# A two-layer float32 hybrid decoder: the indexer's queries and keys turned by VectorE and DRAM instead of TensorE, and four waits moved

## The chip, the cores and the metric

The kernel runs on one core of a Trainium2 chip. The metric is the device time of one execution in microseconds (us). Three runs of the kernel before gave 906.01, 906.24 and 907.55 us, a median of 906.24. The profile is of a further execution.

## The reference, cut to what matters

Two layers with an RMSNorm, one wide input projection, two kinds of attention heads, a gate and an output projection each. The sequence has 256 positions and the model 2048 columns. In layer 0 a small indexer with 16 heads of 64 columns (`iq`, `ik`) scores the keys of every query; the best 64 keys are what the heads of mixer A may attend to.

```python
def dsa_attention(q, k, v, iq, ik, iw):              # mixer A, layer 0
    dots = einsum('bqhd,bsd->bqhs', iqb, ikf) * IDX_DIM ** -0.5
    score = einsum('bqh,bqhs->bqs', iwb * IDX_HEADS ** -0.5, relu(dots))
    score = where(causal, score, -inf)
    _, sel = top_k(score, 64)
    ...                                              # softmax attention over the selected keys

def stick_breaking_attention(q, k, v):               # mixer C, layer 1
    z = einsum('bqhd,bshd->bhqs', qb, k) * HEAD_DIM ** -0.5
    log_1m = where(before, log_sigmoid(-z), 0.0)
    tail = cumsum(log_1m, axis=3, reverse=True) - log_1m
    w = where(before, exp(log_sigmoid(z) + tail), 0.0)
    return einsum('bhqs,bshd->bqhd', w, v)

def forgetting_attention(q, k, v, log_f):            # mixer D, layer 1
    c = cumsum(log_f, axis=1)
    logits = einsum(q, k) * HEAD_DIM ** -0.5 + (c[t] - c[s])
    return softmax(causal(logits)) @ v

def layer_even(x, norm_g, w_in, w_out):              # layer_odd likewise with C, D and log_f
    h = rmsnorm(x, norm_g)
    qa, ka, va, iq, ik, iw, qb, kb, vb, gate = split_cols(h @ w_in)
    qa, ka, iq, ik, qb, kb = rope of each            # halves turned against each other
    y = concat(dsa_attention(...), dilated_attention(...))
    return x + (y * silu(gate)) @ w_out
```

## The kernel before, in words

The program is a row of 39 jobs, each a projection of 256 tokens by up to 512 columns: B0, K, I0, I1, B1 to B3, A0 to A8, B4, B5 (layer 0's input), P0 to P3 (its output), C0, F1, G1, C2 to C7, D0 to D7, and Q0 to Q3. I0 and I1 are the indexer's queries, eight heads each; K holds the shared key and value of mixer A and the indexer's key. F1 and G1 together are head C1 and the forget gates.

A weight in float32 is split in two by ScalarE (`whi`, line 283) and VectorE (`wlo`, line 284), 128 x 1024 elements (a "half", two of the 16 blocks of 128 model columns) at a time, three halves ahead of TensorE, in four buffers each. TensorE then makes six 128 x 512 matmuls for each of the 16 blocks (lines 324, 325, 327): high by high, high by low, low by high, for both halves of the tokens. One such block is a **tick** of the program's clock (`tick`, `advance`).

All else is written as Python generators that say `yield n`: go on n ticks later. `start` sets one off when the projection it needs is done. So the order of the instructions of every engine is fixed when the program is built, and a step that is reached before its input is there makes its engine wait, with everything behind it.

Data is turned (tokens in partitions to tokens in columns) in two ways. `turn` (line 385) lets TensorE do it: a transpose of 128 x 128 each, into a PSUM tile `tp`, out of which ScalarE and VectorE copy. `far` (lines 410 to 432) goes another way: VectorE turns the 32 x 32 blocks of a tile (line 416), a DMA stores that to DRAM (line 424), and a second DMA loads it with the blocks in their places (line 426); its three numbers are the ticks before each of the three steps. The queues for these DMAs and for the weights (`raw`) are SyncE's.

The generators that matter here:

- `keys_a` (line 621) begins 4 ticks after K's projection. It rotates both keys; the indexer's key is copied to have it twice side by side (line 629), and `turn` is used on it (line 633). The key of mixer A goes through `far`, two blocks wide.
- `index` (line 648) rotates the queries of eight heads with `rotate`, and uses `turn` four transposes at a time for each half of the tokens (line 657): 8 transposes in I0 and 8 in I1. Then, one tick apart, 8 groups of products `s` (lines 442 to 444, 679, 680) of 3 or 4 matmuls, each followed by ScalarE's Relu (`rl`) and VectorE's sums (`score`).
- `best` (line 691) follows I1's `index`: 16 steps, 2 ticks apart, each taking the 8 largest scores and striking them out; then the mask `nbA` for mixer A's heads.
- `stick_head` (line 882), heads C0 to C7: products of q and k, four functions on ScalarE and VectorE, products with the triangle `tris`, then `z` (line 903), its exponential (904), the split `ph`, `pl` (lines 455, 456), and 4 ticks after the triangle's products `weigh_out` (line 486): products `o` of the weights with the values (442 to 444, 491).
- `forget` (line 845): log of the forget gates, and 13 ticks later its sums over positions (lines 859, 860), in the same single PSUM tile `s` that the heads use.
- `softmax_head` (line 528), heads B and D. The last of each kind (B5 and D7) have their inputs turned by TensorE.

Of the kernel before, what the change touches and what calls it, by code (L numbers as in the profile page):

```python
# [59 lines left out]
def _cols0(n):  # L60
    qa, ka, va, iq, ik, iw, qb, kb, vb, g = O0
    h = int(n[1:] or 0)
    if n == "K":
        p = [_inter(ka, HD), _run_of(va, 0), _inter(ik, DI), np.arange(iw, iw + NI)]
    elif n[0] == "I":
        p = [_inter(iq + (8 * h + i) * DI, DI) for i in range(8)]
    elif n[0] == "B":
        p = [_inter(qb + h * HD, HD), _inter(kb + h * HD, HD), _run_of(vb, h),
             (_run_of if h == HB - 1 else _gate_of)(g, HA + h)]
    else:  # L70
        p = [_inter(qa + h * HD, HD), _inter(qa + (h + 1) * HD, HD), _gate_of(g, h), _gate_of(g, h + 1)]
    return np.concatenate(p)
# [53 lines left out]

CW = 1792
RW = 1280


def _consts():
    q = np.arange(P)[:, None]
    k = np.arange(P)[None, :]
    f = np.float32
    tri = (q <= k).astype(f)
    one = np.ones((P, P), f)
    ntri = -(q >= k).astype(f)
    caus = np.where(k <= q, 0.0, BIG).astype(f)
    nmask = np.concatenate([caus, np.zeros((P, P), f), caus], 1)

    def dil(d):
        c = (d >= 0) & (d <= 128)
        c = c.astype(np.int64) + ((d >= 0) & (d % 4 == 0)) + ((d >= 0) & (d % 16 == 0))
        return np.where(c > 0, -np.log(np.maximum(c, 1).astype(np.float64)), BIG).astype(f)

    bmask = np.concatenate([dil(q - k), dil(q + P - np.arange(SEQ)[None, :])], 1)
    sm = np.where(q < k, 0.0, -BIG).astype(f)
    smask = np.concatenate([sm, np.zeros((P, P), f), sm], 1)
    return np.ascontiguousarray(np.concatenate([np.eye(P, dtype=f), tri, one, ntri, -one, nmask, bmask, smask], 1))


def _rope():
    f = np.float32
    pos = np.arange(SEQ).astype(f)

    def tab(dim):
        half = dim // 2
        inv = (f(10000.0) ** (-np.arange(half, dtype=f) / f(half))).astype(f)
        ang = pos[:, None] * inv[None, :]
        c, s = np.cos(ang).astype(f), np.sin(ang).astype(f)  # L160
        return np.repeat(c, 2, 1), np.stack([-s, s], -1).reshape(SEQ, dim)

    c, s = tab(HD)
    sc = f(-(HD ** -0.5))
    t = np.concatenate([c * sc, c, s * sc, s], 1).astype(f)
    ci, si = tab(DI)
    t = np.concatenate([t, ci, si], 1)
    return np.ascontiguousarray(t.reshape(NT, P, -1).transpose(1, 0, 2).reshape(P, -1))
# [5 lines left out]
def trunk(ctx, tc, x, xT, g1, w0, wo0, w1, wo1, bf, gf, consts, rope, out):  # L174
# [22 lines left out]
    ones = cons[:, 256:384]  # L197
    ntri = cons[:, 384:512]
    nones = cons[:, 512:640]
    nmask = cons[:, 640:1024]  # L200
    bmask = cons[:, 1024:1408]
    smask = cons[:, 1408:1792]
    ss = cp.tile([P, 3, NT, 5], F32, name="ss")
# [162 lines left out]
    def rotate(dst, src, cos, sin, r, m, swap=False):  # L366
# [15 lines left out]
        else:  # L382
            nc.gpsimd.tensor_tensor(dst, t1[:, 0:n], t2[:, 0:n], op=OP.add)  # L383

    def turn(srcs):
        pt = pa.tile([P, 512], F32, name="tp", tag="tp", bufs=2)
        for i, s in enumerate(srcs):
            nc.tensor.transpose(pt[:, i * P:(i + 1) * P], s, ident)  # L388
        return pt
# [14 lines left out]
    def arrived(t, n):  # L404

        return t.rearrange("p (i b c) -> p b i c", i=4, b=n)
# [121 lines left out]
    def softmax_head(qk, ticks, nb, v, u, rs, kt, last):  # L528
        uT = None if last else gate_turned(u)
        qk = yield from qk_turned(qk, ticks, last)  # L530
        pr, l = soft(qk, nb() if callable(nb) else nb)
        yield 2
        share(pr, factor(l, rs))
        yield 2 if last else 4
        pt = turn([pr[:, 0:P], pr[:, P:SEQ], pr[:, SEQ:384]])
# [87 lines left out]
    def keys_a(ps):  # L623
        kr = hp.tile([P, 512], F32, name="kr", tag="qk")
        for th in range(NT):
            rotate(kr[:, th * P:(th + 1) * P], ps[th][:, 0:P], rt[:, th, P:2 * P], rt[:, th, 3 * P:4 * P], 1, P)
            o = 256 + th * P
            rotate(kr[:, o:o + DI], ps[th][:, 256:320], rt[:, th, 512:576], rt[:, th, 576:640], 1, DI)
            nc.gpsimd.tensor_copy(kr[:, o + DI:o + P], kr[:, o:o + DI])
            nc.scalar.activation(vA[:, 1 - th, :], ps[1 - th][:, P:2 * P], AF.Copy, scale=r0[:, 1 - th:2 - th])  # L630
            nc.vector.tensor_scalar(iw[:, th, :], ps[th][:, 320:336], r0[:, th:th + 1], None, op0=OP.mult)
        yield 5
        pt = turn([kr[:, i * P:(i + 1) * P] for i in (2, 3)])
        nc.scalar.activation(ikh[:, 0:SEQ], pt[:, 0:256], AF.Copy)
        nc.vector.tensor_tensor(ikl[:, 0:SEQ], pt[:, 0:256], ikh[:, 0:SEQ].bitcast(F32), op=OP.subtract)
        for j in range(2):
            d = slice(j * DI, (j + 1) * DI)
            c = slice(SEQ + j * P, SEQ + (j + 1) * P)
            for t in (ikh, ikl):
                nc.gpsimd.tensor_copy(t[d, c], t[d, 0:P].bitcast(F32))  # L640
        yield from far([kr[:, 0:256]], kr[:, 0:256], 1, 2, 4)
        yield 5
        k = arrived(kr[:, 0:256], 2)
        nc.scalar.activation(quarters(kA), k[:, 0:1], AF.Copy)
        nc.scalar.activation(quarters(kAh), k, AF.Copy)
        nc.vector.tensor_tensor(quarters(kAl), k, quarters(kAh).bitcast(F32), op=OP.subtract)

    def index(ps, c):
# [4 lines left out]
        for th in range(NT):  # L653
            rotate(qr[th], ps[th], rt[:, th, 512:576], rt[:, th, 576:640], 8, DI)
        yield 3
        for th in range(NT):
            pt = turn([qr[th][:, i * P:(i + 1) * P] for i in range(4)])
            if th == 0:
                nc.scalar.activation(ih[:, 0], pt, AF.Copy)
                nc.vector.tensor_tensor(ih[:, 1], pt, ih[:, 0].bitcast(F32), op=OP.subtract)  # L660
            else:
                pq = pt.rearrange("p (a b) -> p a b", a=4)
                d = [slice(0, DI), slice(DI, P)]
                for j in range(2):
                    nc.scalar.activation(il[d[j], :, j], pq[d[j]], AF.Copy)
                for j in range(2):
                    nc.vector.tensor_tensor(il[d[1 - j], :, j], pq[d[j]], il[d[j], :, j].bitcast(F32), op=OP.subtract)
            yield 2
        for h2 in range(4):
# [174 lines left out]
    def forget(ps):  # L844
# [11 lines left out]
        nc.vector.scalar_tensor_tensor(flat(logf), flat(z), 0.0, flat(e), op0=OP.min, op1=OP.subtract)  # L856
        yield 13
        pc = pa.tile([P, 512], F32, name="s", tag="s", bufs=1)
# [23 lines left out]
    def stick_head(qk, v, uT, kt):  # L882
# [24 lines left out]
        cut((ph, pl), z[:, P:384])  # L907
        yield 4
        weigh_out(ph, pl, z[:, 0:P], v, uT, kt, True)
# [75 lines left out]
    for ji, (_, _, name, _) in enumerate(jobs):  # L985
# [8 lines left out]
        if name == "P0":  # L994
# [6 lines left out]
            tris = [tt[:, 0], tt[:, 1]]  # L1001
            nc.scalar.activation(tris[0], ntri, AF.Copy)
            nc.scalar.activation(tris[1], nones, AF.Copy)
        if name in ("D2", "D4"):
# [5 lines left out]
        elif k == "K":  # L1010
            start(delay(keys_a(ps), 4))
        elif k == "I":
# [53 lines left out]
```

## Time and profile before

| | |
|---|---|
| three runs | 906.01, 906.24, 907.55 us |
| the profiled execution, device time | 905.67 us |
| its span in the profile | 903.9 us |
| mean granted clock of TensorE, of full speed | 0.998 |
| TensorE matmul busy | 892.9 us, 99% |
| TensorE weight load busy (beside the matmuls) | 747.0 us, 83% |
| VectorE busy | 646.8 us, 72% |
| ScalarE busy | 475.0 us, 53% |
| GpSimd busy | 50.5 us, 6% |
| DMA | 194.2 MB, mean 215 GB/s |

How to read it: a matmul's own duration is its time from first to last element through the engine, and the next one starts before it ends. So what a matmul costs the stream is the distance from its start to the start of the next one, not its duration. In the timeline of an engine each row gives the start, the duration, the engine, the line, the instruction and, in brackets, how long the engine stood idle before it and for what. Rows of the same kind that follow each other are merged (x2, x3).

### The profile page before, as it was taken

How to read it: one execution, taken by the hardware profiler on the slowest of the kernel's cores; microseconds unless marked ns; L12 is line 12 of the kernel's file. 1: busy time of each engine (PE TensorE's matmuls, PEld its weight loads, DVE VectorE, ACT ScalarE, POOL GpSimd, SP SyncE). 2: the span in 40 equal slices, each digit the busy share in tenths (PEclk: the TensorE clock that was granted, in tenths of full speed). 3: DMA queues.
4: the chain of work that ended last, by engine and by line, in shares of the span. 5: the costliest groups of instructions: out<-in, count | busy, mean ns of one | idle time of the engine just before them, and what ended most of it. 6: DMA issues, size and time to landing. Idle time of an engine off the chain costs nothing.

```text
span 903.9 us, 11930 instructions
## 1 busy us (share of the span) xinstructions
PE 892.9 (99%) x4295; PEld 747.0 (83%) x4295; DVE 646.8 (72%) x1136; ACT 475.0 (53%) x834; POOL 50.5 (6%) x71
## 2 busy tenths in 40 slices
PE   9999999999999999999999999999999999999996
PEld 6988888888888888888897888888888888887886
DVE  7667888866777776666666777777787777776563
ACT  7645554554555455555455555555555555555440
POOL 0031100000000000000000000000000000001110
PEclk9999999999999999999999999999999999999999
DMA  9884455665555665666576655555676766664542
GB/s 358 333 292 145 182 210 184 227 228 203 201 206 202 215 222 186 233 233 233 165 273 240 208 202 193 206 211 195 211 254 222 238 218 216 205 199 180 188 185 93
DMA packets 67355, 194.20 MB, mean 215 GB/s; under 512 B 15952, under 2 KB 38624, under 8 KB 49376
## 3 DMA queue, kind: packets, MB, share of 16 engines
q1 hardware_dynamic: 65856, 190.14, 59.4%
q0 software_dynamic: 864, 2.12, 1.0%
q10 hardware_dynamic: 576, 1.19, 0.4%
q8 instruction: 33, 0.54, 0.2%
q14 instruction: 26, 0.21, 0.1%
HBM read 178.61 MB, written 14.82 MB: 214 GB/s over the span
## 4 chain that ended last, share of the span: by engine, by line
PE 82%; DVE 10%; ACT 4%; issue 3%; DMA 1%; POOL 0%; SPq 0%; POOLq 0%; DVEq 0%; ACTq 0%
PE pj L324 26%; PE pj L325 25%; PE pj L327 25%; DVE wlo L284 3%; DVE e L834 2%; ACT whi L283 1%; PE tp L388 1%; PE o L443 1%; PE s L504 1%; DVE far L416 1%; DMA w0yh<-in_w_in_dram 1%; PE o L491 1%; PE s L444 1%; PE s L443 1%; PE s L442 1%
## 5 line engine op out<-in xcount | busy, mean ns | idle before, releaser
L284 DVE TENSOR_TENSOR wlo<-raw,whi 128x1024 fp32r<-128x1024 f32 (+3 forms) x300 | 355.1, 1201 | 144.5 <-ACT whi L283 143.7
L324 PE MATMUL pj<-whi,xh 128*128 128x512 f32 (+3 forms) x992 | 381.0, 386 | 0.4 <-ACT whi L283 0.4
L325 PE MATMUL pj<-whi,xl 128*128 128x512 f32 (+3 forms) x992 | 376.5, 381 | 0.0
L283 ACT ACTIVATE whi<-raw 128x1024 fp32r<-128x1024 f32 (+3 forms) x300 | 299.6, 1024 | 85.3 <-PE pj L325 69.6
L327 PE MATMUL pj<-wlo,xh 128*128 128x512 f32 (+3 forms) x992 | 296.9, 381 | 0.1
L324 PEld LDWEIGHTS pj<-whi,xh 128*128 128x128 f32 x992 | 186.7, 188 | 33.3 <-ACT whi L283 1.4
L327 PEld LDWEIGHTS pj<-wlo,xh 128*128 128x128 f32 x992 | 183.4, 188 | 36.6 <-DVE wlo L284 0.8
L325 PEld LDWEIGHTS pj<-whi,xl 128*128 128x128 f32 x992 | 186.7, 188 | 32.0
L324 PE MATMUL pj<-whi,yh 128*128 128x512 f32 (+1 forms) x248 | 95.7, 386 | 0.0
L325 PE MATMUL pj<-whi,yl 128*128 128x512 f32 (+1 forms) x248 | 94.9, 383 | 0.0
L327 PE MATMUL pj<-wlo,yh 128*128 128x512 f32 (+1 forms) x248 | 76.6, 382 | 0.0
L512 ACT ACTIVATE sn<-sn,nm 128x128 f32<-128x128 f32 (+1 forms) x48 | 21.5, 449 | 62.6 <-DVE nm L510 62.6
L327 PEld LDWEIGHTS pj<-wlo,yh 128*128 128x128 f32 x248 | 46.6, 188 | 9.2
L324 PEld LDWEIGHTS pj<-whi,yh 128*128 128x128 f32 x248 | 46.7, 188 | 8.7
L325 PEld LDWEIGHTS pj<-whi,yl 128*128 128x128 f32 x248 | 46.6, 188 | 8.7
L455 ACT ACTIVATE yh<-uT 128x256 fp32r<-128x256 f32 (+1 forms) x27 | 12.4, 458 | 54.8 <-DVE uT L497 28.0
L548 ACT ACTIVATE sq<-xs 128x512 f32<-128x512 f32 x23 | 14.3, 623 | 28.9 <-DVE xs L773 26.9
L834 DVE RECIPROCAL e<-e 128x256 f32<-128x256 f32 x16 | 28.1, 1753 | 0.5
L383 POOL TENSOR_TENSOR qk<-rot,rot 128x256 f32<-128x256 f32 x16 | 11.9, 741 | 227.6 <-DVE rot L378 116.9
L456 DVE TENSOR_TENSOR yl<-uT,yh 128x256 fp32r<-128x256 f32 (+1 forms) x27 | 12.8, 475 | 14.3 <-ACT yh L455 14.3
L871 POOL DMA_DIRECT2D cb<-cTd x8 | 5.8, 722 | 252.2 <-DVE nb L876 223.7
L904 ACT ACTIVATE z<-z 128x384 f32<-128x384 f32 x8 | 4.2, 525 | 29.1 <-DVE z L903 29.1
(229 smaller groups left out, 739.6 us busy)
## 6 DMA issues: line engine op xcount, KB each, us to landing
raw<-in_w_in_dram SPq DMA_DIRECT2D x108, 1024.0 KB, 5.2
raw<-in_w_out_dram SPq DMA_DIRECT2D x32, 1024.0 KB, 4.9
fard<-far SPq DMA_DIRECT2D x38, 256.0 KB, 2.1
qk<-fard SPq DMA_DIRECT2D x25, 256.0 KB, 5.1
raw<-in_w_in_dram SPq DMA_DIRECT2D x4, 672.0 KB, 8.8
fard<-far SPq DMA_DIRECT2D x21, 128.0 KB, 3.7
uT<-fard SPq DMA_DIRECT2D x20, 128.0 KB, 5.0
raw<-in_w_in_dram SPq DMA_DIRECT2D x4, 528.0 KB, 3.8
```

Of the source, the lines that this page charges most:

```text
L283: nc.scalar.activation(hi, rw, AF.Copy)
L284: nc.vector.tensor_tensor(lo, rw, hi.bitcast(F32), op=OP.subtract)
L324: nc.tensor.matmul(o, a, wh, start=(kt == 0), stop=False)
L325: nc.tensor.matmul(o, b, wh, start=False, stop=False)
L327: nc.tensor.matmul(o, a, wl, start=False, stop=(kt == KT - 1))
L383: nc.gpsimd.tensor_tensor(dst, t1[:, 0:n], t2[:, 0:n], op=OP.add)
L443: nc.tensor.matmul(o, ah, bl, start=False, stop=False)
L455: nc.scalar.activation(dst[0], src, AF.Copy)
L456: nc.vector.tensor_tensor(dst[1], src, dst[0].bitcast(F32), op=OP.subtract)
L512: nc.scalar.activation(sn[:, s], sn[:, s], AF.Exp, scale=-1.0, bias=nm[:, th:th + 1], accum_out=l[:, th:th + 1])
L548: nc.scalar.activation(j, xs[:, th, c * 512:(c + 1) * 512], AF.Square, accum_out=ss[:, i, th, c:c + 1])
L834: nc.vector.reciprocal(e, e)
```

## The change

The indexer no longer uses `turn`. Its queries and its key take the way of `far`. For that, the columns of two heads (64 each) are interleaved by 16 in the weights, so that a tile of 128 columns holds a pair and the blocks come out in their places; the tables of the rotation are laid out likewise (128 columns in place of 64: the table `rt` grows by 128 KB, and the constants shrink by as much, two matrices fewer). The key, which has to stand in both halves of the pair, is rotated twice at once by a new function `rotate_twice`. The key of mixer A and that of the indexer go through one `far` of four blocks.

```diff
@@ _cols0
     elif n[0] == "I":
-        p = [_inter(iq + (8 * h + i) * DI, DI) for i in range(8)]
+        p = [_inter(iq + (8 * h + i) * DI, DI).reshape(4, 16) for i in range(8)]
+        p = [np.stack(p[i:i + 2], 1).reshape(-1) for i in range(0, 8, 2)]
...
-CW = 1792
-RW = 1280
+CW = 1536
+RW = 1536
...
+    def rotate_twice(dst, src, cos, sin):
+        t1 = hp.tile([P, 512], F32, name="rot1", tag="rt1")
+        t2 = hp.tile([P, 512], F32, name="rot2", tag="rt2")
+        wide = lambda a: a.rearrange("p (j a m) -> p j a m", j=4, a=2)
+        pair = lambda a: a.rearrange("p (j a m two) -> p j a m two", j=4, a=2, two=2)
+        sb = src.rearrange("p (j m) -> p j m", j=4).unsqueeze(2).to_broadcast([P, 4, 2, 16])
+        nc.vector.tensor_tensor(wide(t1[:, 0:P]), sb, wide(cos), op=OP.mult)
+        sw = src.rearrange("p (j m two) -> p j m two", j=4, two=2)[:, :, :, ::-1]
+        for a in range(2):
+            nc.vector.tensor_tensor(pair(t2[:, 0:P])[:, :, a], sw, pair(sin)[:, :, a], op=OP.mult)
+        nc.gpsimd.tensor_tensor(dst, t1[:, 0:P], t2[:, 0:P], op=OP.add)
@@ softmax_head
         pr, l = soft(qk, nb() if callable(nb) else nb)
-        yield 2
+        if not last:
+            yield 2
         share(pr, factor(l, rs))
-        yield 2 if last else 4
+        yield 4
@@ keys_a
-            rotate(kr[:, o:o + DI], ps[th][:, 256:320], rt[:, th, 512:576], rt[:, th, 576:640], 1, DI)
-            nc.gpsimd.tensor_copy(kr[:, o + DI:o + P], kr[:, o:o + DI])
+            rotate_twice(kr[:, o:o + P], ps[th][:, 256:320], rt[:, th, 512:640], rt[:, th, 640:768])
...
-        yield 5
-        pt = turn([kr[:, i * P:(i + 1) * P] for i in (2, 3)])
-        nc.scalar.activation(ikh[:, 0:SEQ], pt[:, 0:256], AF.Copy)
...
+        yield from far([kr], kr, 2, 2, 4)
+        yield 4
+        k = arrived(kr, 4)
+        nc.scalar.activation(quarters(ikh[:, 0:SEQ]), k[:, 2:4], AF.Copy)
...
-        yield from far([kr[:, 0:256]], kr[:, 0:256], 1, 2, 4)
-        yield 5
...
@@ index
         for th in range(NT):
-            rotate(qr[th], ps[th], rt[:, th, 512:576], rt[:, th, 576:640], 8, DI)
-        yield 3
+            rotate(qr[th], ps[th], rt[:, th, 512:640], rt[:, th, 640:768], 4, P)
         for th in range(NT):
-            pt = turn([qr[th][:, i * P:(i + 1) * P] for i in range(4)])
...
-            yield 2
+            start(far([qr[th]], qr[th], 2, 2, 4))
+        yield 12
+        hi, lo = (quarters(ih[:, j]) for j in range(2))
+        nc.scalar.activation(hi, arrived(qr[0], 4), AF.Copy)
+        nc.vector.tensor_tensor(lo, arrived(qr[0], 4), hi.bitcast(F32), op=OP.subtract)
+        yield 2
+        pq = arrived(qr[1], 4)
...
+        yield 4
         for h2 in range(4):
@@ forget
-        yield 13
+        yield 15
@@ stick_head
         cut((ph, pl), z[:, P:384])
-        yield 4
+        yield 5
         weigh_out(ph, pl, z[:, 0:P], v, uT, kt, True)
@@ before P0
-            nc.scalar.activation(tris[0], ntri, AF.Copy)
-            nc.scalar.activation(tris[1], nones, AF.Copy)
+            nc.vector.scalar_tensor_tensor(tris[0], tri, -1.0, ident, op0=OP.add, op1=OP.subtract)
+            nc.scalar.activation(tris[1], ones, AF.Copy, scale=-1.0)
...
         elif k == "K":
-            start(delay(keys_a(ps), 4))
+            start(delay(keys_a(ps), 2))
```

Where the instructions stand now. TensorE in the projection C2, where the forget gates' sums (`s<-logf`) and the values' products of head C0 (`o`) are; `pj` with its number is the tile of one half of the tokens. Before:

```order
L859 MATMUL s<-logf,cons 128x16
L860 MATMUL s<-logf,cons 128x8
L324 MATMUL pj_4581<-whi,xh 128x512
L325 MATMUL pj_4581<-whi,xl 128x512
L324 MATMUL pj_4582<-whi,xh 128x512
L325 MATMUL pj_4582<-whi,xl 128x512
L327 MATMUL pj_4581<-wlo,xh 128x512
L327 MATMUL pj_4582<-wlo,xh 128x512
L442 MATMUL o<-ph,v 128x256
L443 MATMUL o<-pl,v 128x256
L444 MATMUL o<-ph,v 128x256
L491 MATMUL o<-z,v_4237 128x128
```

The same place after (the lines have other numbers: 323, 324 and 326 are the six of a tick, 454 to 456 and 503 the values' products, 870 and 871 the sums):

```order
L323 MATMUL pj_4578<-whi,xh 128x512
L324 MATMUL pj_4578<-whi,xl 128x512
L323 MATMUL pj_4579<-whi,xh 128x512
L324 MATMUL pj_4579<-whi,xl 128x512
L326 MATMUL pj_4578<-wlo,xh 128x512
L326 MATMUL pj_4579<-wlo,xh 128x512
L454 MATMUL o<-ph,v 128x256
L455 MATMUL o<-pl,v 128x256
L456 MATMUL o<-ph,v 128x256
L503 MATMUL o<-z,v_4234 128x128
L870 MATMUL s<-logf,cons 128x16
L871 MATMUL s<-logf,cons 128x8
```

The products `o` stand one tick later than before, in all eight C heads, and the sums two ticks later, right behind C0's `o`.

VectorE in the job Q0, head D7: `sn` are its exponentials, `sc` one over their sum. Before:

```order
L510 ISA sn,nm<-s,nb 128x256
L510 ISA nm 128x1
L284 TENSOR_TENSOR wlo<-raw,whi 128x1024
L497 TENSOR_TENSOR uT<-o,uT 128x2x4x32
L456 TENSOR_TENSOR yl<-uT,yh 128x256
L518 RECIPROCAL sc<-l 128x2
L526 TENSOR_SCALAR sn<-sn,sc 128x128
L526 TENSOR_SCALAR sn<-sn,sc 128x256
```

After:

```order
L522 ISA sn,nm<-s,nb 128x256
L522 ISA nm 128x1
L530 RECIPROCAL sc<-l 128x2
L538 TENSOR_SCALAR sn<-sn,sc 128x128
L538 TENSOR_SCALAR sn<-sn,sc 128x256
L283 TENSOR_TENSOR wlo<-raw,whi 128x1024
L509 TENSOR_TENSOR uT<-o,uT 128x2x4x32
L468 TENSOR_TENSOR yl<-uT,yh 128x256
```

The division of D7's weights stands ahead of the next split and of D6's output instead of behind them; B5's moves likewise. TensorE's transposes of these weights stay at their tick.

VectorE behind the rotation of I0's queries (`iqr`), during the job I1. Before:

```order
L456 TENSOR_TENSOR pl<-tp,ph 128x256
L284 TENSOR_TENSOR wlo<-raw,whi 128x1024
L660 TENSOR_TENSOR ih<-tp,ih 128x512
L497 TENSOR_TENSOR uT<-o,uT 128x2x4x32
L456 TENSOR_TENSOR yl<-uT,yh 128x256
L284 TENSOR_TENSOR wlo<-raw,whi 128x1024
L646 TENSOR_TENSOR kAl<-kr,kAh 128x256
L667 TENSOR_TENSOR il<-tp,il 64x4x128 x2
```

After:

```order
L468 TENSOR_TENSOR pl<-tp,ph 128x256
L428 STREAM_TRANSPOSE far<-iqr 128x4x4x32 x2
L283 TENSOR_TENSOR wlo<-raw,whi 128x1024
L509 TENSOR_TENSOR uT<-o,uT 128x2x4x32
L468 TENSOR_TENSOR yl<-uT,yh 128x256
L283 TENSOR_TENSOR wlo<-raw,whi 128x1024 x4
L670 TENSOR_TENSOR ih<-iqr,ih 128x512
L283 TENSOR_TENSOR wlo<-raw,whi 128x1024
L678 TENSOR_TENSOR il<-iqr,il 64x4x128 x2
```

Two block turns come in, and the queries are split five to six halves later instead of one or two. The 16 groups of products and sums of the indexer, and the 16 steps of `best` behind them, all stand 11 ticks later.

## Rows read from the trace of the kernel before

**Rows 1.** The page's first part: busy us, share of the span, instructions.

```profile
PE 892.9 (99%) x4295; PEld 747.0 (83%) x4295; DVE 646.8 (72%) x1136; ACT 475.0 (53%) x834; POOL 50.5 (6%) x71
```

**Rows 2.** Waits of TensorE and its weight loads: us, times, longest.

```profile
PE s L859 <- DVE z L903: 0.9, 1, 0.9
PE tp L388 <- DVE sn L526: 0.8, 1, 0.8
...
PEld o L443 <- DVE pl L456: 1.9, 7, 0.3
PEld o L442 <- ACT ph L455: 1.9, 7, 0.3
```

**Rows 3.** The indexer's transposes by tile: duration in ns min/median/max, first and last start.

```profile
L388 PE MATMUL tp<-cons,iqr x16: 270/272/273, 69.5 to 99.9; 128*128 128x128 f32 x16
```

**Rows 4.** TensorE's timeline around one turn of four in I1.

```profile
67.68 0.63 PE L327 MATMUL pj<-wlo,xh 128*128 128x512 f32 x2
...
69.05 0.62 PE L327 MATMUL pj<-wlo,xh 128*128 128x512 f32 x2
69.51 0.60 PE L388 MATMUL tp<-cons,iqr 128*128 128x128 f32 x4
...
70.88 0.62 PE L327 MATMUL pj<-wlo,xh 128*128 128x512 f32 x2
```

**Rows 5.** TensorE's timeline: forget gates' sums and C0's values, in job C2.

```profile
480.44 0.73 PE L327 MATMUL pj<-wlo,xh 128*128 128x512 f32 x2
482.04 0.40 PE L859 MATMUL s<-logf,cons 128*128 128x16 f32 x2 [0.87 <-DVE z L903]
...
483.96 0.28 PE L442 MATMUL o<-ph,v 128*128 128x256 f32 x1
...
484.45 0.48 PE L324 MATMUL pj<-whi,xh 128*128 128x512 f32 x1
```

**Rows 6.** TensorE's timeline around C1's values, in job C3.

```profile
505.91 0.62 PE L327 MATMUL pj<-wlo,xh 128*128 128x512 f32 x2
...
507.73 0.39 PE L442 MATMUL o<-ph,v 128*128 128x256 f32 x1
...
508.67 0.48 PE L324 MATMUL pj<-whi,xh 128*128 128x512 f32 x1
```

**Rows 7.** VectorE's timeline at the same place.

```profile
503.85 2.35 DVE L284 TENSOR_TENSOR wlo<-raw,whi 128x1024 fp32r<-128x1024 f32 x2
...
507.71 0.42 DVE L456 TENSOR_TENSOR pl<-z,ph 128x256 fp32r<-128x256 f32 x1 [1.04 <-ACT ph L455]
```

**Rows 8.** TensorE's timeline: D6's and D7's weights turned, in job Q0.

```profile
810.54 0.49 PE L388 MATMUL tp<-cons,sn 128*128 128x128 f32 x3
810.79 0.48 PE L324 MATMUL pj<-whi,yh 128*128 128x512 f32 x1
...
819.82 0.61 PE L327 MATMUL pj<-wlo,yh 128*128 128x512 f32 x2
821.28 0.61 PE L388 MATMUL tp<-cons,sn 128*128 128x128 f32 x3 [0.84 <-DVE sn L526]
821.72 0.38 PE L388 MATMUL tp<-cons,u 128*128 128x128 f32 x2
```

**Rows 9.** VectorE's timeline at the same place.

```profile
818.27 1.23 DVE L284 TENSOR_TENSOR wlo<-raw,whi 128x1024 fp32r<-128x1024 f32 x1 [1.66 <-ACT whi L283]
...
820.85 0.55 DVE L526 TENSOR_SCALAR sn<-sn,sc 128x128 f32<-128x128 f32 x2
```

**Rows 10.** VectorE's 32 x 32 turns, grouped by line and shape: busy us, mean ns.

```profile
L416 DVE STREAM_TRANSPOSE far<-qk 128x512 f32<-128x512 f32 x25 | 17.7, 709 | 0.5
```

**Rows 11.** Busy us of each engine in two stretches of 25 us, clock, DMA.

```profile
70.00:95.00 25.00, 25.00 (x130) 21.05 (x129) 20.99 (x34) 13.99 (x23) 5.08 (x7) 1.00 0.46 165
...
145.00:170.00 25.00, 25.00 (x118) 20.84 (x117) 21.75 (x54) 12.31 (x24) 1.48 (x2) 1.00 0.60 200
```

**Rows 12.** One split of I1's weights on VectorE, and TensorE where it is used.

```profile
57.35 1.18 DVE L284 TENSOR_TENSOR wlo<-raw,whi 128x1024 fp32r<-128x1024 f32 x1
...
65.97 0.62 PE L327 MATMUL pj<-wlo,xh 128*128 128x512 f32 x2
```

**Rows 13.** DMA issues of the way over DRAM: count, KB each, us to landing.

```profile
qk<-fard SPq DMA_DIRECT2D x25, 256.0 KB, 5.1
```

## What the change should do, predicted before it ran

> **What bounds the kernel now.** First the page's busy shares [rows 1]: TensorE has matmuls in flight in 99% of the span, VectorE is at 72%, ScalarE at 53%. A pipelined engine that looks busy may still be held up, so the next view is what TensorE and its weight loads waited for [rows 2]. The list is short: one wait of 0.9 us for `z` before the forget gates' sums, one of 0.8 us for `sn` before the last transposes, and seven pairs of small waits of at most 0.3 us each before the values' products `o`, for `ph` from ScalarE and `pl` from VectorE. Nothing else in some 850 us of steady work. So the kernel's time is TensorE's stream: a matmul taken out of it is time won, a wait taken out of it is time won, and work on another engine costs nothing as long as its result is there when TensorE comes to it.
>
> How far ahead are the others? Counting splits and ticks in order (314 splits of VectorE, 656 ticks, none missing) pairs each `wlo` with its first use. In I1 the first `wlo` is done at 57.35 + 1.18 = 58.53 and used at 65.97 [rows 12], 7.4 us later, and no half of I1 has under 7. In the C heads the fourth half is the tight one: the first of two splits merged in [rows 7] ends at 503.85 + 2.35 / 2 = 505.0 and is used at 505.91 [rows 6], 0.9 us later. So the indexer's stretch has a cover of about 7 us, and the C heads one of under 1 us.
>
> **The change part by part.** What it costs or gives is read from distances between starts in TensorE's timeline.
>
> *Transposes out.* The tick without a turn takes 69.05 - 67.68 = 1.37 us, the next one, with a turn of four in it, 70.88 - 69.05 = 1.83 [rows 4]. A turn of four costs 0.46 us. There are 16 transposes of the queries [rows 3], four turns, and half a turn for the key: 4.5 x 0.46 = 2.1 us.
>
> The mean duration of one such transpose is 0.27 us [rows 3], but four of them, with what they do to the tick behind them, cost 0.46. The Trainium skill, TensorE: Matmul & The Clock Gate, section "Part 4: PE-mode transpose", gives about 275 ns for one in a kernel's context. As a duration the trace agrees (272 ns); as a price per transpose it would make 18 x 0.275 = 4.95 us (an estimate from that page) in place of 2.1.
>
> *The values' products of the C heads, one tick later.* C1's block of `o`, from its first matmul to the next tick, takes 508.67 - 507.73 = 0.94 us [rows 6]; C0's, which came late and found everything ready, 484.45 - 483.96 = 0.49 [rows 5]. The difference, 0.45 us, is waiting: `pl` is made from 507.71 to 508.13 [rows 7], while TensorE wanted it at about 507.85. The head recurs seven times with this wait [rows 2]: 7 x 0.45 = 3.15 us. One tick later is 1.36 us later, at about 509.1, a full microsecond behind the end of `pl`. What moves with it: VectorE's `uT` and `yl` and ScalarE's `yh` go behind the next split, which is then made earlier, not later; the next reader of VectorE's queue, the next head's `qkl`, is wanted by TensorE only some ticks later. The tight fourth half lies ahead of the moved block in each head and hangs on the head's own first products, so it keeps its 0.9 us.
>
> *Forget gates, two ticks later.* The tick's last pair starts at 480.44 and, at 0.23 us a matmul, ends its issue at 480.90; the sums start at 482.04 [rows 5]. That is 1.14 us of waiting for the single PSUM tile `s`, which VectorE frees with `z`. Two ticks later it has long been free: 1.14 us won. C0's `o`, now between them, then comes at about 483.6 and not at 483.96, close behind its `pl`; between 0 and 0.3 us may come back there, and I take 0.
>
> *Last heads.* In Q0 the pair of 819.82 ends its issue at 820.28, and the transposes of D7's weights start at 821.28; the three take 821.72 - 821.28 = 0.44 against 810.79 - 810.54 = 0.25 for D6's [rows 8]. Waiting: 1.00 + 0.19 = 1.19 us. VectorE came to `sn` only at 820.85, behind a split and D6's output, and ahead of that split it had stood idle for 1.66 us, waiting for ScalarE [rows 9]. The division and the two scalings, under 1 us, now fall into that idle time and end by about 818.2, two microseconds before TensorE wants them. 1.19 us won, and no split is later. B5 moves the same way, but it had no wait: 0.
>
> *Added on VectorE.* Five turns of 0.71 us [rows 10], 3.5 us, and for the key and the wider table a few instructions more, at most another 1 us by the same row's 0.71 for 512 columns: 3.5 to 4.5 us. In the stretch from 70 to 95 us VectorE is busy for 20.99 of 25, from 145 to 170 for 21.75 [rows 11]. The indexer's sums and the steps of `best` move 11 ticks, so the end of `best` reaches into A0, on top of that job's own work. The cover of 7 us and idle time of 3 to 4 us in every 25 hold this: 0. If the cover were gone, it would cost those 3.5 to 4.5 us.
>
> The Trainium skill, VectorE: DVE Perf Modes, section "Rules for kernel authors", advises TensorE for a 128 x 128 transpose if PSUM will do as its destination. That speaks against this change. In [rows 1] it is TensorE that has no time left, so by the trace the rule has the wrong engine here; it would be right if VectorE became the bound, which is the first rival.
>
> *Added DMAs.* Each half of the queries is stored and loaded, 256 KB each way, four times. In the stretch concerned the DMA engines are busy at 0.46 [rows 11]. The load is issued at tick 8 and wanted by ScalarE at tick 12, 4 x 1.36 = 5.5 us later; such loads land after 5.1 us [rows 13], and two go together, so ScalarE may wait 0 to 3 us, with its splits behind it and 7 us of cover for those. The indexer's products are wanted only at tick 18. On SyncE's queue a store waits for VectorE's turn, and weights stand behind it, three tiles of which are loaded ahead: 0. The rotation of K, two ticks earlier, runs where VectorE has nothing else: 0, or a small gain.
>
> *Sum.* 2.1 + 3.15 + 1.14 + 1.19 = 7.6 us. The profiled execution took 905.67 us, so it would take 898.1. The median of the three runs is 0.57 us above that, and the forecast is for such a median: 906.24 - 7.6 = 898.7 us (rounded from 898.66).
>
> **The rivals.**
>
> *VectorE becomes the bound between I1 and A0.* For it: the added turns, the later end of `best`, a VectorE that is busy for 87% there. Against it: the cover, which refills in each job. All of the added work would come back: 898.7 + 4.5 = 903.2 us. By the skill's rule just named this is where it would go.
>
> *The C heads' wait only moves.* Taking 0.45 us out of a head brings TensorE sooner to the next thing that is just in time, the fourth half with 0.9 us. If it lost there what it won, 898.7 + 3.15 = 901.8 us.
>
> *The page's price.* If a transpose cost its whole duration, 18 x 0.272 = 4.9 us by [rows 3], the time would be 898.7 - 2.8 = 895.9 us. Against it: the two ticks of [rows 4], which show the cost whole.
>
> *Slower: the queries come too late over DRAM.* ScalarE stands at tick 12 in front of the load, and the splits of the weights stand behind it. Up to a landing of 5.5 us nothing happens; up to 5.5 + 7.4 = 12.9 us the cover pays; beyond that TensorE waits for every microsecond, once in I0 and once in I1. To lose more than the 7.6 us that are won, each landing must take over 12.9 + 3.8 = 16.7 us, three times what [rows 13] shows. At 18 us the time would be 898.7 + 2 x 5.1 = 908.9 us.
>
> **How the numbers follow.** The forecast, all four terms within a microsecond in sum, 0.72. VectorE as the bound, in part or whole, 0.11; the C heads' wait moved, 0.07; the page's price, 0.03; slower, 0.03; the gains there and about as much lost in places I don't see, 0.04. The time given is that of the forecast, 898.7. The range goes from 897.0, a microsecond and the scatter of the runs below it, to 902.2, which takes in half of the first rival and all of the second: about 0.84 of the chance. This kernel's measurement can tell about 0.2%, 1.8 us, from no change. Faster than 904.4 us are the forecast, the C heads' rival, the page's price and the first rival: 0.93. Within 0.2%: 0.04. Slower: 0.03.
>
> **What would show it.** In the profile after: 18 transposes fewer; no wait of TensorE for `z`, none for `sn`, and no pairs of waits for `ph` and `pl`; blocks of `o` in the C heads at 0.49 us; the last transposes 0.25 us for three; VectorE some 4 us busier. The forecast is wrong if TensorE shows new waits for `whi` or `wlo` between 90 and 180 us, for `il` or `ih` ahead of the indexer's products, or for `wlo` in each C head.

## The result, and the profile after

The changed kernel takes 899.83 us, the median of four runs (898.86 to 900.81), against 906.43 for four runs of the kernel before beside it: a ratio of 0.9925, with a 95% interval of 0.9908 to 0.9942. The forecast was 898.7 us, the range 897.0 to 902.2. The profiled execution took 900.81 us, 4.86 less than that of before, where 7.54 were forecast. The first part of the page (busy us, share, instructions; before: [rows 1]):

```profile
PE 888.9 (99%) x4277; PEld 744.9 (83%) x4277; DVE 649.6 (72%) x1143; ACT 474.6 (53%) x833; POOL 50.1 (6%) x69
```

18 transposes are gone. VectorE has 2.8 us more, where 3.5 to 4.5 were forecast. What was added comes close to the forecast all the same: the four turns of the queries take 2.8 us (4 x 694 ns, below), and the key's turn and rotation 0.9 more than before. But the splits `wlo`, the same work in both kernels, take 352.6 us by this page where they took 355.1, which hides part of it. What TensorE waited for (us in total, times, longest), to be held against [rows 2]:

```profile
PE pj L323 <- ACT whi L282: 1.4, 2, 1.0
PE s L987 <- DVE mhalf L983: 1.2, 1, 1.2
```

The waits for `z`, `sn`, `ph` and `pl` are no longer there. The second line is the warming up ahead of the first job, 1.2 us before too. The first, in which the projection itself waits for ScalarE's high parts, stood in the trace of before with one short wait, in the first job:

```profile
PE pj L324 <- ACT whi L283: 0.4, 1, 0.4
```

The wait of 1.0 us is new. Where that is, and the four terms, TensorE's timeline shows (start, duration, what, idle before). C2, to be held against [rows 5]:

```profile
467.37 0.40 PE L326 MATMUL pj<-wlo,xh 128*128 128x256 f32 x2
...
468.09 0.40 PE L326 MATMUL pj<-wlo,xh 128*128 128x256 f32 x2
468.33 0.40 PE L323 MATMUL pj<-whi,xh 128*128 128x512 f32 x1
...
470.88 0.62 PE L326 MATMUL pj<-wlo,xh 128*128 128x512 f32 x2
472.47 0.50 PE L323 MATMUL pj<-whi,xh 128*128 128x512 f32 x1 [0.96 <-ACT whi L282]
...
484.20 0.28 PE L454 MATMUL o<-ph,v 128*128 128x256 f32 x1
...
484.77 0.29 PE L870 MATMUL s<-logf,cons 128*128 128x16 f32 x2
...
485.14 0.48 PE L323 MATMUL pj<-whi,xh 128*128 128x512 f32 x1
```

The forget gates' sums follow the products `o` without a pause. But C2's own weights come late: after the pair of 470.88, whose issue ends at 471.34, TensorE starts again at 472.47. C3, against [rows 6], and D6's and D7's weights in Q0, against [rows 8]:

```profile
507.99 0.62 PE L326 MATMUL pj<-wlo,xh 128*128 128x512 f32 x2
508.45 0.28 PE L454 MATMUL o<-ph,v 128*128 128x256 f32 x1
...
508.94 0.48 PE L323 MATMUL pj<-whi,xh 128*128 128x512 f32 x1
...
816.05 0.62 PE L326 MATMUL pj<-wlo,yh 128*128 128x512 f32 x2
816.51 0.49 PE L400 MATMUL tp<-cons,sn 128*128 128x128 f32 x3
816.83 0.38 PE L400 MATMUL tp<-cons,u 128*128 128x128 f32 x2
```

The block of `o` takes 508.94 - 508.45 = 0.49 us, the three transposes 816.83 - 816.51 = 0.32 and start right behind the pair.

The ledger, from the starts of the 39 jobs in both traces: the first jobs +0.16 us (they differ by up to 1.2 us from run to run), the indexer with K and I0 to B2 -2.14, **C2 +1.34** (27.24 in place of 25.90 us), the seven heads C1 to C7 -0.44 each, together -3.09 (they show in the jobs C3 to D1), Q0 -1.10; in sum -4.9. Everything is as forecast but C2, which should have been 1.1 us shorter. So 2.4 us are lost there, almost 300 us behind the indexer. The experiments are about that.

The places where the forecast feared a loss show none. VectorE's turns and the loads of the queries (us busy, mean ns, and for a load its KB and us to landing):

```profile
L428 DVE STREAM_TRANSPOSE far<-iqr 128x512 f32<-128x512 f32 x4 | 2.7, 694 | 0.2 <-POOL iqr L382 0.2
iqr<-fard SPq DMA_DIRECT2D x4, 256.0 KB, 5.9
```

The loads take 0.8 us longer than [rows 13], and the cover of I1 falls from 7 us to 5.7 at its lowest (`wlo` ready to first use). In A0 it is 4.1, where it was 3.4.

### The profile page after: what moved, and what is told of

Its sections match the earlier page's. It is cut to its first block, busy times and chain, and to the rows that moved or that the text cites. A ratio compares the mean times of both kernels' runs of the same rounds, so it can differ in the third digit from the quotient of the medians.

```text
span 899.0 us, 11923 instructions
## 1 busy us (share of the span) xinstructions
PE 888.9 (99%) x4277; PEld 744.9 (83%) x4277; DVE 649.6 (72%) x1143; ACT 474.6 (53%) x833; POOL 50.1 (6%) x69
## 3 DMA queue, kind: packets, MB, share of 16 engines
q10 hardware_dynamic: 576, 1.19, 0.4%
## 4 chain that ended last, share of the span: by engine, by line
PE 93%; DMA 2%; issue 2%; DVE 2%; ACT 1%; POOL 0%; POOLq 0%; DVEq 0%; SPq 0%; ACTq 0%
PE pj L323 29%; PE pj L326 29%; PE pj L324 29%; DMA raw<-in_w_in_dram 1%; PE tp L400 1%; DVE wlo L283 1%; DMA w0yh<-in_w_in_dram 1%; PE s L516 1%; PE o L503 1%; PE s L455 1%; PE s L454 1%; PE s L456 1%; PE o L454 0%; PE o L456 0%; PE o L455 0%
## 5 line engine op out<-in xcount | busy, mean ns | idle before, releaser
L283 DVE TENSOR_TENSOR wlo<-raw,whi 128x1024 fp32r<-128x1024 f32 (+3 forms) x300 | 352.6, 1194 | 142.7 <-ACT whi L282 141.8
```

The costliest lines, as they stand in the source:

```text
L283: nc.vector.tensor_tensor(lo, rw, hi.bitcast(F32), op=OP.subtract)
```

## The experiments

All of these ran against the kernel before, 905.8 to 906.2 us in each group. The first jobs scatter by more than some of the effects, so the job C2 is read from each trace beside the time.

**Which part of the change makes C2 late?** Four kernels: the changed one again, its indexer alone, its three moved waits alone, and the C heads' wait alone.

> The changed kernel once more, five rounds. Theory 1 (the sum of the prediction holds, and job C2 lost some 2 us because the first weights of C2 landed late in that execution, by the chance of DMA timing): the runs fall into two groups, near 898.9 us without the late weights and near 900.7 with them, and in a profile without them C2 takes about 24.8 us instead of 27.2. Theory 2 (the change itself makes C2's weights late): every run near 900.7, C2 27.2 us in the profile, three to four waits for whi or wlo at its start.

> The indexer's part alone: queries and key turned by VectorE and DRAM, K two ticks earlier, the waits of the C heads, forget gates and last heads as before. By the prediction 2.1 us less: 904.3 against 906.4. Rival (VectorE becomes the bound between I1 and A0): 904.3 to 908.8. Rival (the page's price of a transpose): 901.5. Theory 2 on C2: the first weights of C2 late, TensorE waiting for whi at its start, and the gain of 2.1 us gone: about 906.

> The kernel before with the moved waits of the C heads, the forget gates and the last heads, and the indexer as it was. By the prediction's terms 3.15 + 1.14 + 1.19 = 5.5 us less: 900.9 against 906.4. If the late weights at C2 come with the new transfers of the indexer (theory 2), C2 takes 24.8 us here; if by chance (theory 1), either 24.8 or 27.2.

> The kernel before with the values' products of the C heads one tick later, nothing else. By the prediction 7 x 0.45 = 3.15 us less: 903.3; the jobs C3 to D1 0.45 us shorter each, and the tight fourth half still 0.9 us ahead. Rival (the wait only moves to the fourth half): no change, 906.4.

The changed kernel: 900.31 us, ratio 0.9932 (0.992 to 0.9945), C2 26.27 us. The indexer alone: 905.68, 0.9993 (0.9984 to 1.0002); up to C2 it leads by 1.84 us, then C2 takes 27.63 and the lead is gone. The moved waits alone: 900.41, 0.9938 (0.9926 to 0.9951), C2 24.80: 1.10 us for the forget gates, 0.44 for each C head, 1.10 in Q0. The C heads' wait alone: 903.29, 0.9969 (0.9957 to 0.9982), C2 25.91. C2 is late in all three traces with the new indexer and in none of the three without it, and the indexer's part, as the kernel stands, gives next to nothing. The times alone would not have ruled out theory 1: of the nine runs of the changed kernel three took 898.4 to 899.0 us and six 899.8 to 900.8, and what C2 took in those three no trace shows. So C2's lateness comes with the new indexer, but perhaps not in every execution.

**DRAM buffers?** The indexer's five transfers shift the turn in which the second layer uses the four DRAM buffers of `moved`. One kernel shifts it back, another, with (4, 1) and (2, 3), shifts it in the kernel with the moved waits alone:

```diff
+            for m, c in ((4, 3), (2, 1)):
+                for _ in range(c):
+                    dr.tile([P, P * m], F32, name="fard", tag=f"fard{m}", bufs=4)
```

> The changed kernel, with four buffers passed over at the start of the second layer, so that the transfers over DRAM use there the same DRAM buffers in turn as in the kernel before. Instructions and their waits are as in the changed kernel. Theory A (the late weights at C2 hang on which of the four DRAM buffers a store or load of the second layer meets): C2 takes 24.8 us as in the kernel with the moved waits alone, its first half of weights is ready over 2 us ahead of TensorE, and the time is 898.6 us. Theory B (they hang on what the indexer's transfers leave behind in another way, or on the lead itself): C2 takes 26.3 to 27.3 us and the time is 900.2 us.

> The kernel before with the three moved waits and the indexer as before, with four buffers passed over, so that the transfers over DRAM use in the second layer the DRAM buffers of the changed kernel. Theory A (buffers): C2 takes 26.3 to 27.3 us in place of 24.8 and the time is 902.2 us. Theory B: C2 stays at 24.8 us and the time at 900.4.

900.15 us and C2 27.10; 901.45 us and C2 24.66. The first is theory B in both numbers: with the buffers of before C2 is late all the same, and theory A falls. The second agrees in C2; its time lies between the two forecasts (its runs go from 900.51 to 904.08, and the one with the trace is a 900.51).

**The lead, or the transfers?** One kernel has the new indexer but as much TensorE work put back behind it, one has TensorE work taken out without the new indexer, one has the transfers beside the old indexer. In this order (`cut_low` is true in B3 for the blocks 3, 5, 7 and 9):

```diff
+    def padding():
+        yield 1
+        for n in (4, 4, 4, 4, 2):
+            turn([ident] * n)
+            yield 2
...
+        if cut_low:
+            return
         for o, a in zip(os, ah):
             nc.tensor.matmul(o, a, wl, start=False, stop=(kt == KT - 1))
...
+        for th in range(NT):
+            start(there_and_back(qr[th]))
```

> The changed kernel with 18 transposes of a constant put into the job B3, four turns of 4 and one of 2, whose results nobody reads: the TensorE work that the change took out is put back behind the indexer, so everything from there on runs at about the times of the kernel before, but the indexer's transfers have been made. By the two ticks of the trace of before it costs 4.5 x 0.46 = 2.1 us. Theory L (the late weights at C2 come of the 1.9 us by which the second layer runs earlier): C2 is as with the moved waits alone, 24.7 us, and the time is 900.4 us, no more than 0.3 us above the changed kernel. Theory H (they come of something that the indexer's transfers leave behind in the queues): C2 stays at 26.3 to 27.3 us and the time is 902.3 us.

> The kernel before with the three moved waits, the indexer as before, and in the job B3 the products of the low parts of the weights left out for 4 of the 16 blocks (8 matmuls of 512 columns, 4 x 0.46 = 1.84 us): a lead of 1.9 us without any change to the transfers. Theory L: C2 takes 26.3 to 27.3 us and the time is 900.2 us, nearly nothing of the 1.84 us being kept. Theory H: C2 stays at 24.7 us and the time is 898.6 us.

> The kernel before with the three moved waits, the indexer's turns on TensorE as before, and beside them the four stores and four loads of 256 KB each that the changed kernel makes for the queries (the loads go to DRAM and are read by nobody). Theory H, that the number of transfers made before matters: C2 26.3 to 27.3 us, the time 902.2 us. Theory L: C2 24.7 us and 900.4 us.

900.93 us and C2 24.84; 899.58 and 24.70; 901.62 and 24.94. With the work put back C2 is on time, although the transfers are made, and with the transfers alone it is on time too: theory H, as it was put, falls. (The 1.2 us by which that last time lies above the moved waits alone stand in the first job.) The padding, started when B3 is done, put 2.08 us into A0, and the time is 0.6 us above that of the changed kernel, where theory L allowed 0.3 and theory H asked for 2.0. But the kernel with work taken out has a lead of 1.0 us at C2 (1.5 won in B3, 0.4 lost in A0) and C2 is on time. Either 1.0 us is not enough, or it is not the lead.

**What lies in DMA at that place.** The weights that are loaded ahead of C2's are G1's, and those are late already. SyncE's DMA issues (start, duration, what), before and then after:

```profile
448.46 0.33 SPq L424 DMA_DIRECT2D fard<-far  x1
449.91 0.33 SPq L257 DMA_DIRECT2D raw<-in_w_in_dram  x1
451.18 0.38 SPq L426 DMA_DIRECT2D qk<-fard  x1
453.86 0.33 SPq L257 DMA_DIRECT2D raw<-in_w_in_dram  x1
456.05 0.33 SPq L424 DMA_DIRECT2D fard<-far  x1
456.47 0.89 SPq L257 DMA_DIRECT2D raw<-in_w_in_dram  x2
...
460.99 0.51 SPq L257 DMA_DIRECT2D raw<-in_w_in_dram  x1
```

```profile
446.48 0.33 SPq L436 DMA_DIRECT2D fard<-far  x1
447.93 0.33 SPq L256 DMA_DIRECT2D raw<-in_w_in_dram  x1
448.51 0.38 SPq L438 DMA_DIRECT2D qk<-fard  x1
451.87 0.33 SPq L256 DMA_DIRECT2D raw<-in_w_in_dram  x1
455.12 0.33 SPq L436 DMA_DIRECT2D fard<-far  x1
455.54 0.89 SPq L256 DMA_DIRECT2D raw<-in_w_in_dram  x2
...
459.10 0.61 SPq L256 DMA_DIRECT2D raw<-in_w_in_dram  x1
```

Up to 451.87 all is 2.0 us earlier or more; then the store and the two loads, which hang on splits of G1's weights, come 1.05 us late against that. The last row of each is C2's first load. It is issued 1.89 us earlier, so it still has nearly the whole lead; what is late is its landing (us, the last number), before and after:

```profile
raw<-in_w_in_dram SPq DMA_DIRECT2D x1, 1024.0 KB, 5.5
```

```profile
raw<-in_w_in_dram SPq DMA_DIRECT2D x1, 1024.0 KB, 7.8
```

These 2.3 us are about what C2 loses. The load of 447.93 is the first of G1's, and it lands late too, before and after:

```profile
raw<-in_w_in_dram SPq DMA_DIRECT2D x1, 512.0 KB, 3.4
```

```profile
raw<-in_w_in_dram SPq DMA_DIRECT2D x1, 512.0 KB, 5.3
```

And in the same microseconds another queue is at work. The page of before lists it as:

```profile
q8 instruction: 33, 0.54, 0.2%
```

33 packets of 0.54 MB / 33 = 16.4 KB: pieces of the program. TensorE has 4295 matmuls and as many weight loads, 8590 / 33 = 260 instructions to a piece; at 12 a tick of 1.36 us that is one every 29 us, and two in a row come at 394.2 and 422.4. The Trainium skill, Runtime: NRT & Kernel Launch, section "Instruction fetch mechanics", says that an engine's instructions are refilled in blocks of 256 (16 KiB) over a DMA queue of its own, and that this is mostly hidden. The trace agrees with the size; the price is the next question. The piece near G1's load, read in stretches of 0.2 us (packets, MB, share of 16 DMA engines). Before, from 448.6:

```profile
q8 instruction: 1, 0.02, 29.1%
```

After, from 449.0:

```profile
q8 instruction: 1, 0.02, 67.2%
```

Before, it takes 0.291 x 0.2 x 16 = 0.9 us of one DMA engine and ends ahead of G1's load, beside the store. After, it begins 1.1 us behind the issue of that load and takes 2.2 us. It has moved because the change takes 36 instructions out of TensorE's stream (18 transposes with their weight loads): the piece is asked for 36 instructions later. In the half-wide jobs a tick with its 12 takes 468.09 - 467.37 = 0.72 us, so by some 2.2 us; 2.4 was seen. In the twelve traces with the usual pieces of weights (the begin to 0.2 us):

| kernel | piece begins, from the issue of G1's first load | that load lands after | C2's first load lands after | C2 |
|---|---|---|---|---|
| before | -1.3 us | 3.4 us | 5.5 us | 25.90 us |
| C heads' wait alone | -1.3 | 3.5 | 5.4 | 25.91 |
| moved waits | -1.3 | 3.4 | 5.5 | 24.80 |
| with other buffers | -1.2 | 3.6 | 5.3 | 24.66 |
| with the transfers | -1.4 | 3.5 | 5.6 | 24.94 |
| work put back | -1.5 | 3.4 | 5.5 | 24.84 |
| work taken out | +0.3 | 4.2 | 5.4 | 24.70 |
| changed kernel, first | +1.1 | 5.3 | 7.8 | 27.24 |
| again | +1.6 | 5.1 | 7.0 | 26.27 |
| with other buffers | +0.8 | 5.1 | 7.8 | 27.10 |
| indexer alone | +1.3 | 5.1 | 7.2 | 27.63 |
| numbers put back (below) | -1.5 | 3.6 | 6.0 | 25.34 |

The two loads go together: where G1's takes over 5 us, C2's takes 7.0 to 7.8. How the one lengthens the other is not shown; between them are G1's last two loads, 1.05 us late. The kernel with work put back has the 36 instructions back as well, and that with work taken out has 16 fewer: the pair that was to tell lead from transfers moved the piece too.

**The piece alone.** The last test moves nothing but the numbers of TensorE's instructions, ahead of the first job, where it waits anyway:

```diff
-    for n in [512] * 8:
+    for n in [256] * 6 + [128] * 20:
         nc.tensor.matmul(pw[:, 0:n], warm[:, 0:P], warm[:, 0:n], start=True, stop=True)
```

> The changed kernel with the 8 warming-up matmuls ahead of the first job, 512 columns each, cut into 26 with the same 4096 columns in all: 18 matmuls and 18 weight loads more, so that TensorE's instructions from the first job on have the numbers that they have in the kernel before. Nothing else changes, and TensorE has nothing to do at that place. Theory F (TensorE's instructions are loaded by DMA in pieces of 256; the change takes 36 of them out, and so the piece that is loaded at about 449 us falls into the load of G1's first weights, 1.1 us behind its issue, where before it lay 1.3 us ahead of it): the piece comes 1.3 us ahead of that load again, C2 takes 24.8 us, and the time is 898.4 us (897.9 to 898.9). Theory L (the earlier time of the second layer by itself): the piece may come earlier, but C2 stays at 26.3 to 27.3 us and the time at 900.3 us.

It took 898.87 us, ratio 0.9918 (0.9904 to 0.9931), 1.44 below the changed kernel's repeat; these two ran beside different runs of the kernel before and their intervals overlap (the first measurement's ratio, 0.9925, is closer still), so the verdict is the trace's. All five of its runs took 897.99 to 899.08. The lead at C2 is the same 2.0 us, the piece is at 446.4 (it has moved with TensorE's numbers, so the queue is TensorE's) and G1's load lands after 3.6 us. The page lists a second queue of such pieces, q14; its piece nearest to this place is at 443.3 to 443.4 us in the changed kernel and in this one. ScalarE's splits of G1's first and C2's first weights (with the idle time before, and what ended it), of the changed kernel and of this one:

```profile
453.38 1.15 ACT L282 ACTIVATE whi<-raw 128x512 fp32r<-128x512 f32 x2 [2.32 <-PE pj L324]
...
467.01 1.06 ACT L282 ACTIVATE whi<-raw 128x1024 fp32r<-128x1024 f32 x1 [4.43 <-DMA raw<-in_w_in_dram]
```

```profile
451.82 0.63 ACT L282 ACTIVATE whi<-raw 128x512 fp32r<-128x512 f32 x1 [0.80 <-DVE wlo L283]
...
465.10 1.06 ACT L282 ACTIVATE whi<-raw 128x1024 fp32r<-128x1024 f32 x1 [2.56 <-DMA raw<-in_w_in_dram]
```

G1's first split is 1.56 us earlier, and C2's first 1.91 (the row that names PE for 2.32 us of idle time is one of those where the last releaser was another: the load issued at 447.93 landed 5.3 us later, at 453.3). Theory F holds for the load and the time, and theory L, which asked for 26.3 to 27.3 us in C2 at this lead, falls. C2 took 25.34 us, not the 24.8 of theory F: its first 1 MB landed after 6.0 us, where the kernels that are on time show 5.3 to 5.6. So the piece accounts for 0.9 to 1.9 us of what C2 loses in the traces of the changed kernel, by one trace without it; the last half microsecond stays open.

**A way around it.** The half-wide jobs F1 and G1 are loaded in four pieces each like the others, so their three buffers hold half as much ahead. With larger pieces C2's weights are asked for at 454.6, not at 459.1:

```diff
-        for n in (FIRST if (first and i == 0) else REST):
+        for n in (FIRST if (first and i == 0) else {264: (6, 6, 4), 256: (8, 8)}.get(w, REST)):
```

> The changed kernel with the weights of the two half-wide jobs F1 and G1 loaded in 3 and 2 pieces in place of 4 each, so that the three buffers reach further ahead and C2's first weights are asked for earlier. If C2 is late because the half-wide jobs leave too little read ahead, then C2's first half is ready over 2 us ahead of TensorE, C2 takes 24.8 us, and the time is 898.4 us (898.0 to 899.0), below both kernels. If the DMA engines' rate at that place is what limits, the weights land no sooner: C2 26 to 27 us and 900.2 us.

> The kernel before with the weights of F1 and G1 loaded in 3 and 2 pieces. With them the changed kernel took 898.1 us and its C2 24.2 us. If the larger pieces only take away the loss at C2, then here, where the first half was ready 2.4 us ahead, they give at most the half microsecond by which C2's fourth half waits: 905.7 to 906.1 us, and the change itself, with the pieces on both sides, is worth 7.6 to 8.0 us. If they bring a gain of their own, it shows here as well: about 904 us.

The changed kernel with them takes **898.09 us** (897.72 to 898.31), ratio 0.9911 (0.9898 to 0.9924), below both kernels; C2 takes 24.21 us, and ScalarE's split of its first weights at 463.54 waits for TensorE and no longer for the load. The piece of instructions still comes at 449.0, but no weights are on their way then. The kernel before with them takes 904.81, 0.999 (0.9981 to 0.9999), and its C2 24.71 in place of 25.90: more than the half microsecond expected, since an earlier C0 also frees the tile of the forget gates' sums sooner (that wait falls from 0.9 to 0.2 us). With the larger pieces on both sides the change is worth 6.7 us, not the 7.6 to 8.0 expected.

## Why the prediction was right, point by point

- *Transposes out, 2.1 us.* The traces give 2.14 from K to B2, and the 18 transposes put back cost 2.08. The price by the Trainium skill, TensorE: Matmul & The Clock Gate, section "Part 4: PE-mode transpose", 4.95 us as estimated from its 275 ns each, did not come; the two ticks of [rows 4] had it whole.
- *C heads, 3.15 us.* 7 x 0.44 = 3.1, alone and in the change. The fourth half kept its cover (0.84 us in both traces); the rival in which the wait moves did not come.
- *Forget gates, 1.14 us.* 1.10 with the moved waits alone. In the changed kernel the term can't be seen, as C2 is longer for another reason.
- *Last heads, 1.19 us.* 1.10 in Q0; the three transposes take 0.32 us, not 0.25.
- *VectorE and the added DMAs, 0.* Right in the places named: no new wait between 90 and 180 us, lowest cover 4.1 us.
- *The step that failed* is the sum's silent one: that what is changed at 40 to 130 us has no price elsewhere. The new indexer costs 1.5 to 2.4 us in C2, which is more than the 1.1 us by which 899.83 lies above the forecast. That the time still lies in the range is luck in this part: the room above the forecast was made for two rivals that did not come. The prediction's signs of failure named whi and wlo between 90 and 180 us and the C heads; the wait for `whi` came at 472 us, in a job whose weights were little ahead already (in the trace of before the second of C2's halves is ready 0.8 us ahead of its use, and the fourth 0.06). That job could have been found: the half-wide jobs ahead of it and the wait of ScalarE for its load, 2.0 us in the trace of before, stood there. The view of [rows 2] has a row more, over which the prediction's "nothing else" goes: `PEld pj L327 <- DVE wlo L284: 0.8, 2, 0.5`; those 0.5 us are the weight load at 480.44 us, in C2, waiting for the fourth half. For cover the prediction had looked at I1 and at C3. That the piece of instructions would move into that load could not have been read from [rows 1 to 13].
- The slower rival, queries late over DRAM, needed landings of 16.7 us; they were 5.9.

## What to carry to other kernels

Measure a repeated operation by the distance between the starts of the ticks with and without it, and a wait by the same block once with and once without it: all four terms came out within 0.1 us. Before adding up, look for the jobs with the least read ahead, far from the change too, since a shift can show there first; more of the weights asked for ahead of such a job paid 1.7 to 2.2 us here for one line, and 1.0 in the kernel before. And when time is lost far from an edit, look at what moves with the number of instructions.

## What was not expected of the hardware

TensorE's own instructions come by DMA in pieces of about 260. Such a piece takes 0.9 us of one DMA engine in the trace of before. Where it came 0.8 to 1.6 us behind the issue of a load of 512 KB, in four traces, that load landed after 5.1 to 5.3 us in place of 3.4 to 3.6; 0.3 us behind the issue it cost 0.8. Moving the piece by 36 instructions, with nothing else changed, brought 3.6 back. That is shown, for this one load.

How 16 KB cost a load of 512 KB up to 1.9 us is shown in part, by its last microseconds (packets, MB, share of 16 DMA engines). The changed kernel, 451.8 to 452.8, and the one with the numbers put back, 450.2 to 451.2, each ahead of the landing:

```profile
q1 hardware_dynamic: 6, 0.02, 6.0%
```

```profile
q1 hardware_dynamic: 326, 0.32, 90.4%
```

A sixteenth is 6.25%: for a whole microsecond the late load keeps no more than one DMA engine's worth of the sixteen busy. The Trainium skill, DMA: Bandwidth & Descriptors, section "Why a DMA increments its semaphore by 16 and not by 1", says that a load is complete only when each of its engines has finished. The trace agrees: the load lands at 453.3, when these last packets are through. That they are on the engine that carried the piece fits, but the trace does not name the engine of a packet.
